# One hybrid block in split fp32: VectorE alone makes the mixer's low weight parts, with deeper weight buffers

## The chip, the core and the metric

The kernel runs on one core of a Trainium2 chip. The metric is the device time of one execution in microseconds. Before the change, three runs took 2448.56, 2450.65 and 2450.76 us; the median is 2450.65 us. The engines are called as the profile calls them: PE (TensorE), DVE (VectorE), ACT (ScalarE), POOL (GpSimd) and SP (the engine whose queue issues the transfers).

## The reference

One transformer block on 256 tokens of width 2048, all in fp32. A vector `c` gives shift, scale and gate for three sublayers: a gated feed-forward network (width 5632), a mixer, and a second feed-forward network. Each result is scaled by its gate, added to the scaled input and normalised. Cut to the core:

```
y = swiglu_ffn(x*(1+scale0)+shift0, ...);  x = layer_norm(ALPHA*x + 0.5*gate0*y)
y = hybrid_mixer(x*(1+scale1)+shift1, ...); x = layer_norm(ALPHA*x + gate1*y)
y = swiglu_ffn(x*(1+scale2)+shift2, ...);  x = layer_norm(ALPHA*x + 0.5*gate2*y)
```

The mixer has two branches. One is differential attention with 8 heads: two softmax maps per head, the second subtracted with a factor. The other is a gated delta rule with 8 heads: a short convolution, a triangular system per chunk of tokens, and a state carried from chunk to chunk. Two gates merge the branches before a last projection.

## The kernel before

**Split products.** Every large weight matrix comes from memory in chunks of 128x1024 fp32 (512 KB, 4 KB in each partition of SBUF). Such a raw chunk `raw` is split into a high part `hi`, which ACT writes by rounding, and a low part `lo = raw - hi`, which is one subtraction of two SBUF tiles (`_split`, lines 177 to 198). Activations are kept as two parts in the same way (`h_hi`, `h_lo`). A product is then three matmuls: hi by hi, lo of the activation by hi, and hi of the activation by lo (`mm3`, lines 145 to 149; L147, L148 and L149 in the profile). One chunk feeds 24 such matmuls of 256 columns, or 12 of 512.

**Buffers.** `RAWB` raw chunks (5) and `WB` pairs of part buffers (3) rotate. `weights` (line 219) is called as PE's instructions for a chunk are written. It first has `ahead` issue the splits of the next `WB - 1` chunks and transfers up to `RAWB` chunks past the last split. A `hi` waits until PE has read the buffer's former content, and a transfer waits until both parts of the raw chunk that it overwrites are made.

**Who makes `lo`.** Line 193 chooses: with `pool_lo` 0 it is DVE, with 1 POOL, with 2 POOL for each even chunk. The value is 1 or 2 in the first visits of the start (`START_LO`), 1 at the change from one sublayer to the next, `POOL_LO` in the mixer (line 1298) and 0 elsewhere.

**The order.** It is written out when the program is built. The main stream of matmuls runs through, and small threads (a convolution, an attention head, a pair of delta-rule heads) put their steps between its products when a clock of the planner, `k.t`, has passed the time at which the planner expects the step's inputs. The planner counts what DVE, ACT and POOL have been given, each on a clock of its own (`_Engine`, lines 75 to 89). So moving an operation from one engine's count to another's also moves the steps of the threads. Each engine runs its instructions in the written order.

**The mixer.** Its main stream makes queries, keys, values, gates and projections (`MIXER_JOBS`, line 41). Beside it four pairs of delta-rule heads (`_delta_pair`) and eight attention heads (`_attn_head`) pass through DVE, ACT and PE in chains of many short steps. `_gates` (line 843) computes decay rates by a chain of small POOL operations (`pol`), then `sp` and `g` on DVE, and then PE multiplies `g` (`pG`). POOL also makes `kqd`, `yal` and `ybl`, the last two being low parts of the branches' results. The branch products that follow the mixer read `ybl`.

**The start.** PE's first visit needs two tiles of activations, which come from vectors of `w_ada` (`sar`) by DVE, ACT and POOL (`_h_tile`, line 493: `hf`, `h_hi`, `h_lo`).

Of the kernel before, what the change touches and what calls it, by code (L numbers as in the profile page):

```python
# [34 lines left out]
DEPTH = 3  # L35
PACE = 2.5
START_LO = (1, 1, 1, 2, 0, 0)
RAWB = 5
WB = 3
MARGIN = 0.9  # L40
MIXER_JOBS = [("d", 0), ("v", 0), ("d", 1), ("a", 0), ("d", 2), ("a", 1), ("d", 3), ("a", 2), ("a", 3)]
POOL_LO = 2
TAIL = 2
LAST_TAIL = 5
MORE0 = 12
# [46 lines left out]
class _Kernel:  # L92
    def __init__(self, tc):
# [10 lines left out]
        self.users = []  # L104
        self.depth = RAWB

# [62 lines left out]
    def _dma(self):  # L169
        i = self.nd  # L170
        self.came[i] = self.load(self.through.get(i - RAWB, 0.0))
        raw = self.rawp.tile([128, 1024], F32, tag="raw", name=f"raw{i}")
# [46 lines left out]
    def weights(self, held=0):  # L219
# [3 lines left out]
        i = self.nu  # L223
        upto, n = i, WB - 1 - held
        while n and upto + 1 < len(self.plan):
# [61 lines left out]
def _xstat(k, n, act, done, tail=0):  # L287
# [21 lines left out]

    more = max(0, tail - WB)  # L310
    if more:
# [975 lines left out]
def _mixer(k, a, h, pre, mk_ada, finish):  # L1287
    nc, tc = k.nc, k.tc
    acts = [h, h]
    with ExitStack() as mctx:  # L1290
# [5 lines left out]
        with tc.tile_pool(name="dp", bufs=1) as dp:  # L1296
            k.dp = dp
            k.pool_lo = POOL_LO
            dv = dp.tile([128, 2, 1024], F32, tag="dv", name="dv")
# [80 lines left out]
def _first_h(k, a, h, hp):  # L1380
# [24 lines left out]
    for i, (f, half, kind) in enumerate(plan):  # L1405
# [13 lines left out]
        if half and kind:  # L1419
# [8 lines left out]
            if f == 3:  # L1428
                k.depth = RAWB


@with_exitstack
def tile_hybrid_block(ctx: ExitStack, tc: tile.TileContext, names, aps):
# [6 lines left out]
    k.pp = pp = ctx.enter_context(tc.tile_pool(name="pp", bufs=1))  # L1440
    k.rawp = ctx.enter_context(tc.tile_pool(name="rawp", bufs=RAWB))
    k.wp = ctx.enter_context(tc.tile_pool(name="wp", bufs=WB))
    k.smallp = ctx.enter_context(tc.tile_pool(name="smallp", bufs=2))
# [262 lines left out]
```

## Time and profile before

| | before |
|---|---|
| median of 3 runs | 2450.65 us |
| the profiled execution | 2450.7 us, span 2448.6 us |
| PE busy | 2341.9 us (96%) |
| DVE busy | 1718.0 us (70%) |
| ACT busy | 1038.1 us (42%) |
| POOL busy | 469.2 us (19%) |
| mean granted PE clock | 0.982 |
| read from memory | 572.98 MB |

The span runs from the first to the last instruction. The stages, by time from the span's start: first feed-forward network to about 790 us, mixer proper about 826 to 1321, branch products and projection to about 1663, second feed-forward network to the end. An engine's busy share is a mean over these stages. A wait is put down to the instruction that ended it.

### The profile page before, as it was taken

The numbers are of one execution on the slowest core, as the hardware profiler recorded it, in microseconds if no ns is written. First come the engines' busy times: TensorE is split into PE (matmuls) and PEld (weight loads), VectorE is DVE, ScalarE is ACT, GpSimd is POOL, SyncE is SP. The second block draws the span as 40 slices with busy tenths as digits, with TensorE's granted clock in tenths as the row PEclk, the third lists the DMA queues.
The fourth block names the chain that finished last, engine by engine and source line by source line (L and its number), as shares of the span: only waits on it lengthen the run. The fifth ranks groups of instructions, "written<-read, shape, count | busy, mean of one in ns | idle before, by whom it ended". The sixth has DMA issues, their size and how long they took to land. (4 is left out here: it accounts for less than half of the span.)

```text
span 2448.6 us, 42378 instructions
## 1 busy us (share of the span) xinstructions
PE 2341.9 (96%) x16989; PEld 2218.5 (91%) x16989; DVE 1718.0 (70%) x2480; ACT 1038.1 (42%) x1420; POOL 469.2 (19%) x276
## 2 busy tenths in 40 slices
PE   7999989999999899989899999998999999999997
PEld 7999987899998779888789999988999988999987
DVE  5767887877765676987876887786786555444456
ACT  4434444344444445444443434444434433444433
POOL 6883000000002532342422210013040000000001
PEclk8999999999999999999999999999999999999999
DMA  9998878998865555444446888875888555555553
GB/s 366 337 332 295 296 237 280 319 335 302 301 219 179 194 175 188 143 164 148 149 151 232 297 305 295 292 273 196 295 310 274 193 194 190 182 186 184 182 194 123
DMA packets 166380, 582.05 MB, mean 238 GB/s; under 512 B 19820, under 2 KB 22812, under 8 KB 165416
## 3 DMA queue, kind: packets, MB, share of 16 engines
q1 hardware_dynamic: 166184, 579.36, 68.1%
q8 instruction: 133, 2.18, 0.4%
q14 instruction: 63, 0.52, 0.1%
HBM read 572.98 MB, written 7.88 MB: 237 GB/s over the span
## 5 line engine op out<-in xcount | busy, mean ns | idle before, releaser
L88 ACT ACTIVATE hi<-raw 128x1024 fp32r<-128x1024 f32 x768 | 811.4, 1059 | 1012.9 <-PE mm L148 406.0
L88 DVE TENSOR_TENSOR lo<-raw,hi 128x1024 fp32r<-128x1024 f32 x631 | 790.2, 1255 | 534.5 <-ACT hi L88 532.6
L149 PE MATMUL mm<-h_hi,lo 128*128 128x256 f32 x3072 | 868.7, 283 | 16.5 <-DVE lo L88 16.4
L147 PE MATMUL mm<-h_hi,hi 128*128 128x256 f32 x3072 | 880.6, 287 | 0.0
L148 PE MATMUL mm<-h_lo,hi 128*128 128x256 f32 x3072 | 871.2, 284 | 0.0
L149 PEld LDWEIGHTS mm<-h_hi,lo 128*128 128x128 f32 x3072 | 585.8, 191 | 18.6 <-DVE lo L88 18.1
L147 PEld LDWEIGHTS mm<-h_hi,hi 128*128 128x128 f32 x3072 | 581.7, 189 | 3.1 <-issue 2.8
L148 PEld LDWEIGHTS mm<-h_lo,hi 128*128 128x128 f32 x3072 | 582.3, 190 | 1.2 <-issue 0.8
L88 POOL TENSOR_TENSOR lo<-raw,hi 128x1024 fp32r<-128x1024 f32 x137 | 337.5, 2470 | 1090.6 <-ACT hi L88 1080.3
L148 PE MATMUL mx<-lo,hid 128*128 128x512 f32 (+1 forms) x764 | 283.3, 371 | 1.5 <-DVE lo L88 1.5
L147 PE MATMUL mx<-hi,hid 128*128 128x512 f32 (+1 forms) x764 | 283.0, 370 | 1.6 <-ACT hi L88 1.6
L149 PE MATMUL mx<-hi,hid 128*128 128x512 f32 (+1 forms) x764 | 282.8, 370 | 0.0
L147 PE MATMUL mms<-h_hi,hi 128*128 128x256 f32 x896 | 253.5, 283 | 9.6 <-ACT hi L88 6.7
L149 PE MATMUL mms<-h_hi,lo 128*128 128x256 f32 x896 | 255.1, 285 | 2.9 <-POOL lo L88 1.6
L148 PE MATMUL mms<-h_lo,hi 128*128 128x256 f32 x896 | 255.1, 285 | 2.2 <-POOL h_lo L88 2.2
L147 PEld LDWEIGHTS mms<-h_hi,hi 128*128 128x128 f32 x896 | 171.6, 192 | 10.4 <-ACT hi L88 7.1
L149 PEld LDWEIGHTS mms<-h_hi,lo 128*128 128x128 f32 x896 | 170.0, 190 | 3.7 <-POOL lo L88 1.9
L148 PEld LDWEIGHTS mms<-h_lo,hi 128*128 128x128 f32 x896 | 169.6, 189 | 2.6 <-POOL h_lo L88 2.5
L147 PEld LDWEIGHTS mx<-hi,hid 128*128 128x128 f32 x764 | 144.0, 188 | 27.2 <-ACT hi L88 2.1
L148 PEld LDWEIGHTS mx<-lo,hid 128*128 128x128 f32 x764 | 143.9, 188 | 26.8 <-DVE lo L88 2.5
L149 PEld LDWEIGHTS mx<-hi,hid 128*128 128x128 f32 x764 | 144.0, 188 | 24.6
L88 DVE SCALAR_TENSOR_TENSOR acc<-ar,cs,acc 128x512 f32<-128x512 f32 x180 | 147.3, 818 | 8.5 <-DMA ar<-in_w_gate_dram 5.0
(295 smaller groups left out, 2530.8 us busy)
## 6 DMA issues: line engine op xcount, KB each, us to landing
raw<-in_w_ffn_in_dram SPq DMA_DIRECT2D x240, 512.0 KB, 4.3
raw<-in_w_ffn_out_dram SPq DMA_DIRECT2D x176, 512.0 KB, 4.1
raw<-in_w_first_dram SPq DMA_DIRECT2D x112, 512.0 KB, 4.8
ar<-in_w_gate_dram SPq DMA_DIRECT2D x96, 512.0 KB, 4.7
ar<-in_w_ada_dram SPq DMA_DIRECT2D x96, 512.0 KB, 4.9
sar<-in_w_ada_dram SPq DMA_DIRECT2D x64, 512.0 KB, 6.0
raw<-in_w_gab_dram SPq DMA_DIRECT2D x64, 512.0 KB, 4.2
raw<-in_w_kq_dram SPq DMA_DIRECT2D x32, 512.0 KB, 3.5
```

Of the source, the lines that this page charges most:

```text
L88: return f(*args, **kw)
L147: mm(ps, lhsT=lhs[0], rhs=rhs[0], start=start, stop=False, skip_group_check=True)
L148: mm(ps, lhsT=lhs[0], rhs=rhs[1], start=False, stop=False, skip_group_check=True)
L149: mm(ps, lhsT=lhs[1], rhs=rhs[0], start=False, stop=stop, skip_group_check=True)
```

## The change

Four numbers. `POOL_LO` goes from 2 to 0, so that in the mixer DVE makes every low part. `WB` goes from 3 to 4 and `RAWB` from 5 to 6. The scratch for descriptors of dynamic transfers is set to 1024 bytes at the program's construction, where the default was used; the two further buffers take 12 KB in each partition.

```
-RAWB = 5
-WB = 3
+RAWB = 6
+WB = 4
...
-POOL_LO = 2
+POOL_LO = 0
...
-    nc = _bacc.Bacc("TRN2", target_bir_lowering=False, num_devices=1)
+    nc = _bacc.Bacc("TRN2", target_bir_lowering=False, num_devices=1, dynamic_dma_scratch_size=1024)
```

The number of POOL instructions falls by 58 and that of DVE grows by 58; in the mixer it is 59, and at the start POOL gets one more. No other instruction is added or removed, but many stand elsewhere.

POOL at the start; `h_lo` is the low part of a tile of activations, `lo` that of a weight chunk. Before:

```order
L88 TENSOR_TENSOR h_lo_89<-hf_178,h_hi_88 128x256
L88 TENSOR_TENSOR lo_185<-raw_165,hi_184 128x1024
L88 TENSOR_TENSOR lo_191<-raw_170,hi_190 128x1024
L88 TENSOR_TENSOR lo_199<-raw_182,hi_198 128x1024
L88 TENSOR_TENSOR h_lo_89<-hf_224,h_hi_88 128x256
L88 TENSOR_TENSOR lo_256<-raw_188,hi_255 128x1024
```

and now:

```order
L88 TENSOR_TENSOR h_lo_89<-hf_178,h_hi_88 128x256
L88 TENSOR_TENSOR lo_185<-raw_165,hi_184 128x1024
L88 TENSOR_TENSOR lo_191<-raw_170,hi_190 128x1024
L88 TENSOR_TENSOR lo_199<-raw_182,hi_198 128x1024
L88 TENSOR_TENSOR lo_205<-raw_188,hi_204 128x1024
L88 TENSOR_TENSOR h_lo_89<-hf_230,h_hi_88 128x256
```

A fourth weight part stands ahead of the second tile's `h_lo`; on ACT its `hi` stands ahead of that tile's `h_hi` likewise.

DVE early in the mixer, where `_gates` ends (`raw` with `ada` is a product of vectors, `v` a convolution, `pG` is PE's). Before:

```order
L88 SCALAR_TENSOR_TENSOR kq_1_8960<-th_9207,kq_1_8960 128x512
L88 ISA raw_9041,ada_9088<-raw_9041,crow,tmp_9089 128x1024
L88 ISA ada_9088 128x1
L88 TENSOR_SCALAR beta<-beta 128x16
L88 SCALAR_TENSOR_TENSOR sp<-xx,pol 128x16
L88 SCALAR_TENSOR_TENSOR g<-sp,ea 128x16
L88 SCALAR_TENSOR_TENSOR v_0_9219<-mm_9036,convw,v_0_9219 128x255 x2
L88 COPY G<-pG 128x16
```

and now:

```order
L88 TENSOR_TENSOR lo_9180<-raw_9012,hi_9179 128x1024
L88 SCALAR_TENSOR_TENSOR kq_1_8968<-th_9229,kq_1_8968 128x512
L88 TENSOR_TENSOR lo_9234<-raw_9048,hi_9233 128x1024
L88 SCALAR_TENSOR_TENSOR v_0_9227<-mm_9044,convw,v_0_9227 128x255 x2
L88 TENSOR_TENSOR lo_9256<-raw_9054,hi_9255 128x1024
L88 TENSOR_SCALAR beta<-beta 128x16
L88 SCALAR_TENSOR_TENSOR sp<-xx,pol 128x16
L88 SCALAR_TENSOR_TENSOR g<-sp,ea 128x16
```

Low parts now stand between the small steps. On PE, `pG` stands 18 matmuls of 512 columns further on in the main stream.

POOL late in the mixer (`yal` is an attention head's low part, `ybl` that of a pair of delta-rule heads). Before:

```order
L88 TENSOR_TENSOR lo_13894<-raw_13689,hi_13893 128x1024
L88 TENSOR_TENSOR lo_14000<-raw_13794,hi_13999 128x1024
L88 TENSOR_TENSOR ybl<-nz_3_13459,ybh 128x512
L88 TENSOR_TENSOR lo_14041<-raw_13891,hi_14040 128x1024
L88 TENSOR_TENSOR yal<-yf_14011,yah 128x256
L88 TENSOR_TENSOR lo_14135<-raw_13965,hi_14134 128x1024
L88 TENSOR_TENSOR yal<-yf_14176,yah 128x256
```

and now:

```order
L88 TENSOR_TENSOR yal<-yf_13522,yah 128x256
L88 TENSOR_TENSOR yal<-yf_13758,yah 128x256
L88 TENSOR_TENSOR yal<-yf_13964,yah 128x256
L88 TENSOR_TENSOR yal<-yf_14200,yah 128x256
L88 TENSOR_TENSOR ybl<-nz_3_13410,ybh 128x512
```

The weight parts are gone from POOL, and the last `ybl` stands behind the last `yal`. On PE the delta rule's steps stand later in the main stream: the second pair's by up to 252 main matmuls, and the last pair's last transposes 87 main matmuls before the branch products where they stood 282 before them.

## Rows read from the trace of the kernel before

**Rows 1.** Windows: start:end length, then busy us of each engine, clock, DMA.
```profile
1700.00:1800.00 100.00, 100.00 (x833) 99.92 (x833) 72.58 (x85) 44.56 (x57) 6.90 (x5) 1.00 0.84 287
826.00:1321.00 495.00, 451.37 (x3409) 425.72 (x3408) 380.18 (x816) 216.84 (x432) 182.44 (x106) 0.97 0.48 164
300.00:370.00 70.00, 60.53 (x439) 56.14 (x438) 62.22 (x95) 32.78 (x57) 0.00 (x0) 0.98 0.74 245
```

**Rows 2.** What PE waited for, 826 to 1321: us, times, longest.
```profile
PE mm L149 <- DVE lo L88: 15.5, 7, 4.6
PE pG L153 <- DVE g L88: 6.9, 1, 6.9
PE UY L153 <- DVE mn L88: 4.1, 1, 4.1
```

**Rows 3.** Groups by form on DVE, 826 to 1321: busy us, mean ns, idle before.
```profile
L88 DVE TENSOR_TENSOR lo<-raw,hi 128x1024 fp32r<-128x1024 f32 x60 | 83.6, 1394 | 50.8 <-ACT hi L88 50.8
L88 DVE TENSOR_TENSOR U<-U,UY 128x512 f32<-128x512 f32 x20 | 13.3, 684 | 2.6 <-PE UY L153 1.9 <-ACT hi L88 0.6
L88 DVE TENSOR_SCALAR r<-r,lam 128x2 f32<-128x2 f32 x8 | 7.8, 977 | 0.3
```

**Rows 4.** The same view on POOL, 826 to 1321.
```profile
L88 POOL TENSOR_TENSOR lo<-raw,hi 128x1024 fp32r<-128x1024 f32 x59 | 149.9, 2542 | 291.8 <-ACT hi L88 281.6 <-PE sc L153 10.2
```

**Rows 5.** The same view on DVE, 1950 to 2350, where POOL is idle.
```profile
L88 DVE TENSOR_TENSOR lo<-raw,hi 128x1024 fp32r<-128x1024 f32 x142 | 174.0, 1226 | 197.7 <-ACT hi L88 197.7
```

**Rows 6.** Instructions in order of time around 851: start, us, engine, idle before.
```profile
850.89 4.63 POOL L88 TENSOR_TENSOR lo<-raw,hi 128x1024 fp32r<-128x1024 f32 x2
850.96 2.29 DVE L88 SCALAR_TENSOR_TENSOR sp<-xx,pol 128x16 f32<-128x16 f32 x1 [1.94 <-POOL pol L88]
853.29 2.26 DVE L88 SCALAR_TENSOR_TENSOR g<-sp,ea 128x16 f32<-128x16 f32 x1
```

**Rows 7.** The same view around 1172.
```profile
1169.60 0.16 DVE L88 SCALAR_TENSOR_TENSOR d_ft<-d_ft,msq 128x4 f32<-128x4 f32 x1
1169.78 2.38 POOL L88 TENSOR_TENSOR lo<-raw,hi 128x1024 fp32r<-128x1024 f32 x1 [2.62 <-ACT hi L88]
1169.80 2.38 DVE L88 SCALAR_TENSOR_TENSOR fa<-d_ft,fa 128x4 f32<-128x4 f32 x1
...
1172.89 2.42 POOL L88 TENSOR_TENSOR lo<-raw,hi 128x1024 fp32r<-128x1024 f32 x1 [0.72 <-ACT hi L88]
1173.03 3.36 DVE L88 TENSOR_TENSOR lo<-raw,hi 128x1024 fp32r<-128x1024 f32 x1
...
1176.44 0.58 PE L149 MATMUL mm<-h_hi,lo 128*128 128x256 f32 x1 [4.65 <-DVE lo L88]
```

**Rows 8.** The same view: the first and the last held instruction of DVE.
```profile
837.26 1.30 DVE L88 SCALAR_TENSOR_TENSOR e<-xx 128x16 f32<-128x16 f32 x1
...
1290.79 1.37 DVE L88 TENSOR_SCALAR ae<-ae,r 128x128 f32<-128x128 f32 x1
```

**Rows 9.** What PE waited for, 300 to 370.
```profile
PE aps L153 <- ACT acchi L88: 3.7, 2, 3.0
PE mx L148 <- DVE lo L88: 1.5, 2, 0.8
```

**Rows 10.** Instructions in order of time at the start.
```profile
20.74 1.06 ACT L88 ACTIVATE hi<-raw 128x1024 fp32r<-128x1024 f32 x1 [2.68 <-DMA raw<-in_w_first_dram]
...
21.70 0.40 ACT L88 ACTIVATE h_hi<-hf 128x256 fp32r<-128x256 f32 x1
21.87 2.34 POOL L88 TENSOR_TENSOR lo<-raw,hi 128x1024 fp32r<-128x1024 f32 x1 [1.37 <-ACT hi L88]
...
24.17 0.72 POOL L88 TENSOR_TENSOR h_lo<-hf,h_hi 128x256 fp32r<-128x256 f32 x1
24.95 0.58 PE L148 MATMUL mms<-h_lo,hi 128*128 128x256 f32 x1 [2.21 <-POOL h_lo L88]
```

**Rows 11.** DMA queues, whole span: packets, MB, share of 16 engines.
```profile
q1 hardware_dynamic: 166184, 579.36, 68.1%
```

## The prediction, made before the changed kernel ran

> **What bounds the kernel now.** I read the windows first, to find where PE loses time. In an undisturbed stretch PE is busy throughout and does 833 matmuls in 100 us, so one of 256 columns costs 0.120 us, at full clock [rows 1]. Outside the mixer most windows look like that one. The mixer does not: of its 495 us PE is busy 451.4, so 43.6 are idle, and its granted clock averages 0.97. With two levels, 2.4 and 1.2 GHz, a mean of 0.97 is 6% of the time at the lower one, and costs 0.03 x 495 = 14.9 us of work. What the mixer can give back by shorter waits is therefore at most 43.6 + 14.9 = 58.5 us. DVE is busy 380.2 us there, 77%, and POOL 182.4.
>
> Second, the waits. PE's 43.6 us in the mixer divide into 15.5 for low weight parts from DVE, 6.9 for `g`, and 21.2 for other steps of the chains, the longest 4.1 [rows 2].
>
> Third, the durations, which tell why DVE is late. Where POOL is idle a `lo` takes DVE 1.226 us [rows 5]; in the mixer the same form has a mean of 1.394 [rows 3]. The order of time shows the reason. `sp` and `g` work on 16 columns and took 2.29 and 2.26 us, while two of POOL's `lo` ran [rows 6]. Around 1172 a step of 4 columns took 0.16 us, and an equal one, begun 0.02 us after a POOL `lo`, took 2.38, as long as that `lo`; next a DVE `lo` took 3.36 beside another, and PE stood 4.65 us [rows 7]. So a DVE instruction that meets a POOL `lo` is held to its end. Between 826 and 1321, 43 DVE instructions beside one took over 0.15 us more than their form does elsewhere, the first at 837, the last at 1291 [rows 8], in sum 77 us. `U<-U,UY`, which reads one operand from PSUM, isn't among them: its mean is 684 ns [rows 3].
>
> The Trainium skill says it as a rule (page "SBUF — State Buffer", section "Who interferes with whom"): GpSimd's port pair is VectorE's second, taken as an exclusive lock for an instruction, and a VectorE instruction with two SBUF inputs needs it against a GpSimd instruction that reads SBUF. The trace agrees (2.38 us beside 2.38). By the rule what is held now would go wholly with those POOL instructions, and DVE's sum below would fall as worked out there.
>
> **The low parts in the mixer.** POOL loses 59 `lo`, 149.9 us [rows 4]. DVE gains 59 x 1.226 = 72.3 us [rows 5] and loses up to 77 of holding, so its busy time goes from 380.2 to about 375.5: no more than before. What changes is when it is late: no step of 0.2 us takes 2.3 any more, except beside POOL's remaining small operations.
>
> **The fourth pair.** The `hi` of a chunk still waits for the same event, PE's last use of an older chunk, since both the buffer it overwrites and the point at which it is issued move by one. But PE wants it one chunk later: 24 matmuls, 24 x 0.120 = 2.9 us more slack for each `lo`. The longest wait, 4.6, has 2.2 + 2.1 of holding in it [rows 7], so with 2.9 more it goes. I count all 15.5.
>
> **`pG`.** `sp` and `g` lose some 2.1 us each, and `pG` stands 18 matmuls of 512 columns later (an estimate from the 0.120 for half the columns: 18 x 0.24, some 4 us). Against that, three `lo` stand before `sp` now, 3.7 us, where a vector product stood; DVE had 1.94 us idle there [rows 6]. The 6.9 goes.
>
> **The other chain steps.** Of their 21.2 us I take two thirds, 14.1. The longest, 4.1 [rows 2], had one held instruction before it; and the order puts the steps later in the main stream than before, by up to 252 matmuls, 30 us. One third stays, since these chains also wait on ACT and PE themselves.
>
> Idle time falls by 15.5 + 6.9 + 14.1 = 36.5. The half-clock time I let fall in proportion: 14.9 x 36.5/43.6 = 12.5.
>
> **What DVE's queue costs.** Nothing before shows 59 more `lo` among chain steps. From below it is 0, because the planner now counts them on DVE's clock and places PE's steps accordingly. From above: 77 us of holding went with 36.5 of idle time that I remove, so 72.3 us of new work, if as unlucky, brings back 34. I take 6, near the lower end, as the nearest row is the undisturbed stretch, where DVE is 73% busy and PE has no idle time [rows 1]. Mixer: -36.5 - 12.5 + 6 = -43.
>
> **300 to 370 us.** PE loses 9.5 idle and 0.02 x 70 = 1.4 of clock; DVE is busy 62.2 of 70 [rows 1]. Waits for `acchi` (3.7) and `lo` are the largest [rows 9]. The two sum products (`aps`) stand 51 and 66 main matmuls later, 6 to 8 us, and the `lo` come a chunk earlier in DVE's queue; but DVE's work is the same and it is nearly full. Bounds 0 and -10.9; I take -5.
>
> **The start.** ACT's third `hi` waited for its raw chunk until 20.74, and `h_hi` followed at 21.70 [rows 10]. Now a fourth `hi` is ahead of `h_hi`, and POOL has a fourth `lo`, 2.34 us, ahead of `h_lo`, for which PE waits until 24.95: +2.4. POOL's lag ends it: were the fourth chunk's landing later still, +4. It isn't won back, since PE has no idle time in the following visits.
>
> **At nothing.** The sixth raw chunk only keeps the transfers' distance, as splits run one chunk earlier. The small scratch: SP issues all transfers, on a hardware queue with 579.36 MB [rows 11]; if the size did touch it, the first stage would suffer, and no row bounds that. The changes between sublayers keep ACT's order. In the last tail, the last chunk's split waits for the same matmuls as before.
>
> Sum: -43 - 5 + 2.4 = -45.6, against the profiled execution's 2450.7, which is the median of the runs (2450.65) within 0.1: about **2406 us**. Its own range is 2390 to 2426, from the bounds of the chain steps (two thirds, give or take one third: 7 us, with clock 10) and of DVE's queue.
>
> **Rivals.**
>
> *Given back at the mixer's end.* The last pair's transposes stood 282 main matmuls before the branch products, 34 us; now 87, 10.4 us. Behind them come a product on DVE, `ybh` on ACT and `ybl` on POOL, which the branch products read. If the chain runs further behind the planner than those 10.4 us allow, PE stands there. For it: the planner puts DVE's small steps at 0.08 us plus a little per column, where those of 4 columns take 0.16 [rows 7]. Against it: the held time that it never counted, 77 us, is gone. Price: half the mixer's gain, 22: 2428.
>
> *All of it.* The mixer's 58.5 and the 10.9 of 300 to 370 go, at +2.4: 2450.7 - 67 = 2384. Against it: the chains also depend on ACT and on PE's own order.
>
> *DVE becomes the mixer's bound (the slower side).* If the holding is not POOL's doing, it stays, and DVE needs 380.2 + 72.3 = 452.5 us. In 300 to 370 DVE was as good as full at 62.2/70 = 0.89 [rows 1]; at that share the mixer takes 452.5/0.89 = 508, 13 more than now: 2450.7 + 13 - 5 + 2.4 = 2461. It decides when less than 12 of the 77 us goes (440/0.89 = 495). Against it: two durations that equal POOL's to 0.02 us [rows 6, 7]. The Trainium skill's page "Perfetto Trace Analysis", section "Optimizing Scalar/DVE Operations", speaks for it: a saturated DVE may be helped by giving work to ScalarE or even GpSimd, the reverse of this change; the same paragraph warns that the shared port may spoil it. This trace shows the spoiling (2.38 us for 0.16).
>
> *No change.* The chains are bound by their own latency, and PE's waits move to other steps of the same pair: 2450.7 - 5 + 2.4 = 2448.
>
> **Chances.** Forecast 0.60, given back 0.15, all of it 0.13, no change 0.06, DVE-bound 0.06. A measurement of this kernel tells about 0.2% (5 us) from no change. Faster 0.88, the same 0.06, slower 0.06. The range that leaves out 2 in 10 is 2384 to 2436.
>
> **What will show it.** Right: in the mixer no DVE step of few columns takes over 1 us, but beside `kqd`, `yal` or `ybl`; DVE's `lo` has a mean near 1.23; DVE is busy about 375 us over a mixer of some 450; PE's waits for `lo` and `g` there are under 3 us together; the clock is at 0.99. At the start PE waits for the second `h_lo` until about 27. Wrong: holds as long as before with POOL idle (DVE-bound), or one long wait of PE for `ybl` before the branch products (given back). New waits for `lo` of some us in the mixer would mean that its queue costs more than 6.

## The result, and the profile after

The changed kernel takes 2417.03 us, the median of four runs (2416.54 to 2420.50), where the kernel before takes 2449.61 beside it (2447.17 to 2450.76). The ratio is 0.9863, with an interval of 0.9849 to 0.9878. The forecast was 2406, with a range of 2384 to 2436. The mechanism was right; the gain was 33 us instead of 45.

The profiled execution took 2417.4 us, with a span of 2415.6, against 2450.7 and 2448.6. To find where the 33 us went I measured both traces at the same events of PE: the first product that follows the first feed-forward network (`pre`), the first branch product (which reads `yah`), and the next normalisation's transpose (`lnt`).

| us | before | after | difference |
|---|---|---|---|
| start to `pre` | 796.7 | 799.5 | +2.8 |
| mixer | 524.3 | 490.6 | -33.7 |
| branches and projection | 345.3 | 342.7 | -2.6 |
| second feed-forward network | 782.0 | 782.6 | +0.6 |

The windows of the trace after, with the columns of [rows 1]: the mixer between the same two events as the 495 us there, the stretch from 300 us, and the branches.

```profile
828.60:1290.40 461.80, 441.98 (x3413) 421.97 (x3412) 373.19 (x875) 215.37 (x432) 33.11 (x47) 0.98 0.52 175
300.00:380.00 80.00, 72.34 (x511) 67.70 (x509) 70.24 (x105) 36.73 (x60) 0.00 (x0) 0.96 0.76 248
1290.10:1632.80 342.70, 335.07 (x2508) 322.09 (x2506) 275.04 (x331) 139.06 (x157) 44.86 (x23) 1.00 0.83 291
```

In the first row DVE has 59 instructions more than before and is busy 7 us less (373.2 against 380.2). PE's idle time is 461.8 - 442.0 = 19.8 us, where it was 43.6. The waits that make it up, in the view of [rows 2]:

```profile
PE sc L153 <- ACT qkT L88: 4.0, 2, 3.4
PE mm L149 <- DVE lo L88: 3.5, 2, 2.9
PE pT L158 <- DVE ae L88: 3.0, 2, 2.6
PE av L153 <- DVE nz L88: 2.6, 1, 2.6
PE pT L158 <- DVE tm L88: 2.4, 1, 2.4
PE v L158 <- DVE v L88: 1.7, 2, 1.0
PE pG L153 <- DVE g L88: 1.0, 1, 1.0
```

Low weight parts fell from 15.5 us to 3.5, `g` from 6.9 to 1.0; the forecast had them under 3 together. The other steps of the chains fell only from 21.2 to 19.8 - 3.5 - 1.0 = 15.3. They are the top of the list now.

DVE's durations, by form in the mixer, as in [rows 3]:

```profile
L88 DVE TENSOR_TENSOR lo<-raw,hi 128x1024 fp32r<-128x1024 f32 x119 | 146.9, 1247 | 41.3 <-ACT hi L88 40.0 <-PE sc L153 1.0
L88 DVE TENSOR_TENSOR U<-U,UY 128x512 f32<-128x512 f32 x20 | 13.4, 684 | 6.4 <-PE UY L153 5.1 <-issue 1.1
```

A `lo` is back at 1.25 us, and `U<-U,UY`, which was never held, hasn't moved. The view of one tile, `r`, gives the least, median and longest duration in ns; the mean of this step was 977 [rows 3]:

```profile
L88 DVE TENSOR_SCALAR r<-r,lam x8: 228/228/229, 986.9 to 1257.5; 128x2 f32<-128x2 f32 x8
```

And the instructions in order of time where `_gates` ends, to be held against [rows 6]:

```profile
852.63 1.23 DVE L88 TENSOR_TENSOR lo<-raw,hi 128x1024 fp32r<-128x1024 f32 x1 [0.52 <-ACT hi L88]
853.77 0.17 DVE L88 TENSOR_SCALAR beta<-beta 128x16 f32<-128x16 f32 x1
856.27 0.18 DVE L88 SCALAR_TENSOR_TENSOR sp<-xx,pol 128x16 f32<-128x16 f32 x1 [2.33 <-POOL pol L88]
856.48 0.17 DVE L88 SCALAR_TENSOR_TENSOR g<-sp,ea 128x16 f32<-128x16 f32 x1
```

`sp` and `g` take 0.18 and 0.17 us where they took 2.29 and 2.26. Count a DVE instruction as held when it runs beside one of POOL's and takes over 0.15 us more than the median of its form in the kernel after. The held time in the mixer is then 4.3 us in 8 instructions, and 79.5 in 48 before. (The prediction's 77 us in 43 are those of them that stand beside a POOL `lo`; of these none is left.)

At the start, in order of time, against [rows 10]:

```profile
20.60 1.06 ACT L88 ACTIVATE hi<-raw 128x1024 fp32r<-128x1024 f32 x1 [2.66 <-DMA raw<-in_w_first_dram]
...
21.73 4.65 POOL L88 TENSOR_TENSOR lo<-raw,hi 128x1024 fp32r<-128x1024 f32 x2 [1.35 <-ACT hi L88]
21.87 1.06 ACT L88 ACTIVATE hi<-raw 128x1024 fp32r<-128x1024 f32 x1 [0.21 <-DMA raw<-in_w_first_dram]
22.83 0.40 ACT L88 ACTIVATE h_hi<-hf 128x256 fp32r<-128x256 f32 x1
...
23.29 0.58 PE L147 MATMUL mms<-h_hi,hi 128*128 128x256 f32 x1 [4.22 <-ACT h_hi L88]
...
26.35 0.72 POOL L88 TENSOR_TENSOR h_lo<-hf,h_hi 128x256 fp32r<-128x256 f32 x1
...
27.12 0.58 PE L148 MATMUL mms<-h_lo,hi 128*128 128x256 f32 x1 [3.25 <-POOL h_lo L88]
```

The fourth `hi` is ahead of `h_hi`, and two `lo` stand before `h_lo`. PE gets it at 27.12 instead of 24.95.

### The profile page after: what moved, and what is told of

Its sections match the earlier page's. It is cut to its first block, busy times and chain, and to the rows that moved or that the text cites. A ratio compares the mean times of both kernels' runs of the same rounds, so it can differ in the third digit from the quotient of the medians.

```text
span 2415.6 us, 42349 instructions
## 1 busy us (share of the span) xinstructions
PE 2331.5 (97%) x16989; PEld 2214.6 (92%) x16989; DVE 1708.3 (71%) x2538; ACT 1036.6 (43%) x1420; POOL 323.1 (13%) x218
## 4 chain that ended last, share of the span: by engine, by line
PE 87%; DVE 7%; issue 2%; ACT 1%; DMA 1%; POOL 1%; DVEq 0%; SPq 0%; ACTq 0%; POOLq 0%
PE mm L147 15%; PE mm L148 15%; PE mm L149 15%; PE mx L149 8%; PE mx L147 8%; PE mx L148 8%; PE mms L148 4%; PE mms L147 4%; PE mms L149 4%; DVE lo L88 2%; DVE acc L88 1%; PE UY L153 1%; DVE x L88 1%; ACT hi L88 1%; PE pre L148 1%
## 5 line engine op out<-in xcount | busy, mean ns | idle before, releaser
L88 DVE TENSOR_TENSOR lo<-raw,hi 128x1024 fp32r<-128x1024 f32 x690 | 855.2, 1245 | 524.6 <-ACT hi L88 516.8
L88 POOL TENSOR_TENSOR lo<-raw,hi 128x1024 fp32r<-128x1024 f32 x79 | 189.9, 2412 | 793.4 <-ACT hi L88 793.4
```

The source lines that it names most:

```text
L88: return f(*args, **kw)
```

## The experiments

Theory: POOL's low parts hold DVE, and ending that is nearly all of the gain; the rest of the change is small. The rivals were that the new written order or the deeper buffers bring it, that DVE's holding isn't POOL's doing, or that POOL's `lo` simply come later than DVE's would (2.54 us for 1.23). Against the last, PE waits for no `lo` of POOL's in the mixer before: every one of its waits for low parts there is for DVE's. The mixer column is the time between the two events of the table above, from each run's trace.

| run | pairs, raw chunks | order planned for | mixer's even `lo` made by | time, us | ratio to before, interval | mixer, us |
|---|---|---|---|---|---|---|
| before | 3, 5 | POOL | POOL | 2449.61 | 1 | 524.3 |
| e4 | 3, 5 | POOL | DVE | 2415.83 | 0.9860, 0.9846 to 0.9875 | 491.2 |
| e1 | 3, 5 | DVE | DVE | 2423.99 | 0.9898, 0.9881 to 0.9914 | 498.9 |
| e2 | 4, 6 | POOL | POOL | 2442.56 | 0.9972, 0.9961 to 0.9983 | 518.0 |
| e5 | 4, 6 | DVE | POOL | 2433.84 | 0.9937, 0.9922 to 0.9952 | 508.6 |
| after | 4, 6 | DVE | DVE | 2417.03 | 0.9863, 0.9849 to 0.9878 | 490.6 |
| e7 | 4, 6 | POOL | DVE | 2407.98 | 0.9828, 0.9812 to 0.9845 | 483.1 |

**e1_dve_only: one number of the change, the maker of the low parts.**

```
-POOL_LO = 2
+POOL_LO = 0
```

> POOL_LO is 0 as in the change; the buffers (5 raw chunks, 3 pairs) and the scratch are those of before. Holding theory (DVE late because it is held beside POOL's low parts; 77 us of held time is the cause of most of the mixer's lost PE time): nearly all of the gain is here, about 2422 us (before less 26, and without the 3 us that the start lost). Order theory (PE waits less because the planner, which now counts these low parts on DVE, places chain steps later): the same here, about 2422. Slack theory (the fourth pair is what takes the waits for low parts away): at most 10 us of gain, about 2440, with waits of PE for lo in the mixer of 12 us or more.

Measured: 2423.99 us, so this alone gives three quarters of the change's gain. Its mixer, in the columns of [rows 1]:

```profile
826.00:1300.00 474.00, 449.03 (x3445) 427.09 (x3445) 374.47 (x876) 219.69 (x435) 33.97 (x47) 0.97 0.53 173
```

PE is idle 25.0 us there, 8.2 of it for low parts in two places (7.0 and 1.2), where the changed kernel, with its fourth pair, has 3.5.

**e2_buffers_only: the change without that number.**

```
-POOL_LO = 0
+POOL_LO = 2
```

> Four pairs, six raw chunks and the small scratch as in the change; POOL still makes each even low part in the mixer. Holding theory: held DVE time stays near 77 us; only PE's waits for lo (15.5 us) shrink, by about two thirds with their clock, against +3 at the start: about 2440. Order theory: the planner's counts are those of before, so about 2446. Slack theory: most of the gain, 2420 to 2425.

Measured: 2442.56. The mixer gains 6.3 us and the start loses 3 (the main stream's 200th matmul at 52.5 us, where it is 49.3 before). DVE is held as before, 79.9 us in 50 instructions.

**e3_scratch_only: the small scratch alone.**

```
-    nc = _bacc.Bacc("TRN2", target_bir_lowering=False, num_devices=1)
+    nc = _bacc.Bacc("TRN2", target_bir_lowering=False, num_devices=1, dynamic_dma_scratch_size=1024)
```

> The kernel before with the scratch for dynamic descriptors at 1024 bytes and nothing else; every engine's order is that of before. Theory (the scratch costs and gains nothing, since SP issues the transfers on a hardware queue): 2450 us, ratio 1.000 within 0.002. Rival (a part of the change's 33 us comes from the scratch, for instance by other tile addresses or by fewer bytes to set up at the start): below 2445.

Measured: ratio 0.9996, interval 0.9986 to 1.0006. It costs and gains nothing that can be measured.

**e4_old_order_dve: only who executes.** The planner still counts the even parts on POOL, so that PE, ACT and SP have the order of before to the last row. In the mixer the instruction itself goes to DVE, at the place where it is written.

```
-        eng.tensor_tensor(lo, raw, hi.bitcast(F32), ALU.subtract)
+        (_As(eng, self.nc.vector) if self.in_mixer else eng).tensor_tensor(
+            lo, raw, hi.bitcast(F32), ALU.subtract)
```

(`_As` sets the engine for the length of the call.)

> Buffers and written order of before to the last instruction, but in the mixer the low parts that stood on POOL are executed by DVE, at the same place in the order; the planner still counts them on POOL. Holding theory: held time falls to under 5 us and DVE's busy time in the mixer stays at about 375 us; PE's idle time there falls from 43.6 to about 22: 2425. Order theory: chain steps stand where they stood and DVE has 59 more instructions that the planner did not count: no gain or a loss, 2445 to 2460. Slack theory: 2450, with more waits for lo.

Measured: 2415.83, as fast as the whole change.

```profile
826.00:1288.00 462.00, 440.58 (x3409) 417.82 (x3408) 371.51 (x875) 216.85 (x432) 33.23 (x47) 0.99 0.55 176
```

DVE does 59 instructions more in 8.7 us less [rows 1]; 4.0 us of it is held. Nothing but the executing engine differs, so that alone gives 34 us; whether by the end of the holding is what e8 and e9 ask. PE is idle 21.4 us here. Of it 8.1 are for low parts and 3.4 for `g`, so the other steps of the chains have 9.9, where the changed kernel has 15.3. Set beside e1, it also shows what the planner's new count does by itself: +8.2 us.

**e5_new_order_pool: the reverse.** The changed kernel with its order, but in the mixer POOL executes the even parts (held time 71.1 us in 55 instructions).

```
-        eng.tensor_tensor(lo, raw, hi.bitcast(F32), ALU.subtract)
+        (_As(eng, self.nc.gpsimd) if self.in_mixer and i % 2 == 0 else eng).tensor_tensor(
+            lo, raw, hi.bitcast(F32), ALU.subtract)
```

> Buffers and written order of the changed kernel to the last instruction, but in the mixer each even chunk's low part is executed by POOL again, at the same place in the order; the planner counts it on DVE. Holding theory: held DVE time is back at 60 to 80 us, and most of the gain is lost: about 2440. Order theory: chain steps stand late enough for held steps too: 2417 to 2424. Slack theory: 2417 to 2422.

Measured: 2433.84, 16.8 us above the changed kernel and 8.7 below e2. About half of the gain is lost, not most of it. So where DVE is held, the order planned for DVE is the better one, by 9 us; where it isn't, it is the worse one, by 8.2 with three pairs (e1 against e4) and 10.0 with four (e6 against e7, below, which share their start). In these runs a plan that expects DVE late paid only where DVE was late.

**e6_start_kept: the old look-ahead at the start, up to the fourth tile of activations.**

```
-        upto, n = i, WB - 1 - held
+        upto, n = i, (2 if self.first else WB - 1) - held
...
-        self.depth = RAWB
+        self.depth, self.first = 5, True
...
             if f == 3:
-                k.depth = RAWB
+                k.depth, k.first = RAWB, False
```

> The changed kernel, but until the second tiles of activations are made only 2 chunks are split ahead and 5 raw chunks loaded ahead, as before the change; from then on 3 and 6. If the start's loss comes from the fourth weight part ahead of the second h_hi and h_lo, PE passes its 20th matmul 3 us earlier and the whole is 3.3 us shorter: 2413.7. Rival: the time is given back where DVE is full (300 to 370 us), so 2416 to 2417.

Measured: 2417.95, no gain. The main stream is only 0.7 us behind before up to 109 us. There the look-ahead has been let go, further splits stand ahead of a later tile's `h_hi`, and PE waits from 60 to 130 us as follows, where it waits for neither in the other two traces:

```profile
PE mms L147 <- ACT h_hi L88: 2.0, 1, 2.0
PE mms L148 <- POOL h_lo L88: 0.4, 1, 0.4
```

After them it is 4.9 us behind. The same loss came later.

**e7_old_order_buffers: the buffers of the change, the start of e6, the mixer planned as for POOL and executed on DVE** (the edits of e6 and e4, and `POOL_LO = 2`).

> The written order of before in the mixer (the planner counts each even low part on POOL), executed by DVE, with four pairs, six raw chunks, the small scratch, and the start's look-ahead of before. The order alone cost 8 us at three pairs (2424.0 against 2415.8). If that is a cost of placing the chain steps too late, it stays with four pairs: 2415.8 less the 7 to 10 us that the buffers gave in the mixer, about 2407. Rival: the fourth pair and the order answer to the same waits, and with four pairs the order does not matter: about 2413, as the changed kernel with its start mended.

Measured: 2407.98, the fastest version, 9 us below the change.

```profile
826.00:1285.00 459.00, 444.63 (x3452) 423.19 (x3451) 372.33 (x877) 217.21 (x434) 33.95 (x47) 0.99 0.55 179
```

PE is idle 14.4 us there, and no wait for low weight parts is left in its list. Against e4 the deeper buffers give 491.2 - 483.1 = 8.1 us of the mixer, both planned for POOL. Against e2, which has these buffers and in the mixer this written order, only who executes differs, and the mixer is 518.0 - 483.1 = 34.9 us shorter: e4's 33.1 once more, with four pairs.

**e8_pool_reads: the holding put back, with nothing depending on it.** e4 with the small scratch, and on POOL, wherever it made a low part, a copy of one column of that chunk's `hi` (to begin at the same event) and then this, which no one reads or waits for:

```
+        k.nc.gpsimd.tensor_copy(k.pace, hi[:, 0:1].bitcast(F32))
+        k.nc.gpsimd.tensor_tensor(k.idle, k.idle, k.idle, ALU.subtract)
```

> Buffers and order of before with the mixer's low parts on DVE (2415.8), the small scratch, and 59 more instructions on POOL that nobody waits for: behind each even hi a copy of one column, then a subtraction of a 128x1024 tile from itself (two reads of SBUF, one write, about as long as a low part). If POOL's reading alone holds DVE, no matter for what data, DVE's small steps take up to 2.4 us again and 15 to 30 us come back: 2430 to 2446. If what cost time was that PE waited for POOL's slow results, nothing comes back: 2415 to 2419.

Measured: 2483.38, ratio 1.0141 (1.0118 to 1.0163): 33 us slower than before, more than expected. The window of its mixer:

```profile
826.00:1354.00 528.00, 460.45 (x3408) 432.39 (x3407) 438.35 (x875) 216.24 (x432) 190.43 (x165) 0.95 0.48 154
```

By form, first on POOL, then on DVE:

```profile
L1727 POOL TENSOR_TENSOR idle<-idle 128x1024 f32<-128x1024 f32 x59 | 121.6, 2061 | 0.2 <-POOL pace L1726 0.2
```

```profile
L88 DVE TENSOR_TENSOR lo<-raw,hi 128x1024 fp32r<-128x1024 f32 x119 | 172.2, 1458 | 48.3 <-ACT hi L88 48.2
```

DVE's instructions are those of e4 and take 67 us longer (438.4 after 371.5); counted as above, 70.7 us of them is held. `g`, 0.17 us long in e4, ends with POOL's idle subtraction, at 856.97 and 856.94:

```profile
855.05 1.89 POOL L1727 TENSOR_TENSOR idle<-idle 128x1024 f32<-128x1024 f32 x1
855.21 1.76 DVE L88 SCALAR_TENSOR_TENSOR g<-sp,ea 128x16 f32<-128x16 f32 x1
```

POOL's own steps (`kqd`, `ybl` and others) also queue behind these 59, so e8 alone doesn't show that it is the reads. e9 has about the same queue.

**e9_pool_writes: the same, but POOL only writes.** In place of the subtraction, two memsets of the idle tile:

```
-        k.nc.gpsimd.tensor_tensor(k.idle, k.idle, k.idle, ALU.subtract)
+        [k.nc.gpsimd.memset(k.idle, 0.0) for _ in range(2)]
```

> As the run before, but instead of the subtraction POOL writes zeros twice into the 128x1024 tile (no read of SBUF, about 1 us each). If only POOL's reads hold a DVE instruction with two SBUF inputs, little comes back: 2416 to 2421. If any use of POOL's port holds DVE, a part in proportion to POOL's busy time comes back: 2428 to 2440.

Measured: 2424.18, between the two forecasts. POOL is as busy as in e8 within 14 us, and the mixer is 498.1 us, not 557.4.

```profile
826.00:1295.00 469.00, 443.93 (x3410) 419.94 (x3409) 379.31 (x875) 216.72 (x432) 176.73 (x224) 0.99 0.54 173
```

```profile
L1727 POOL MEMSET idle<- 128x1024 f32 x118 | 112.5, 953 | 3.4
L1726 POOL COPY pace<-hi 128x1 f32<-128x1 f32 x59 | 36.1, 612 | 269.1 <-ACT hi L88 269.1
```

The held time is 14.0 us in 25 instructions, against 70.7 in 56. What is left isn't mainly the 59 copies, although they read; the trace separates it by the kind of DVE's step. Of the instructions that began while a memset ran, all 31 `lo` took as long as alone, within 0.01 us, and so did the 59 other TENSOR_TENSOR steps. But 15 of 17 TENSOR_SCALAR steps, which work on one tile, were held to the memset's end, 8.0 us in sum. In order of time (the second memset ends at 1213.29):

```profile
1211.28 1.22 DVE L88 TENSOR_TENSOR lo<-raw,hi 128x1024 fp32r<-128x1024 f32 x1
1211.33 1.96 POOL L1727 MEMSET idle<- 128x1024 f32 x2
1212.62 0.69 DVE L88 TENSOR_SCALAR r<-r,lam 128x2 f32<-128x2 f32 x1
```

`r`, 0.228 us alone, ends at 1213.31. Of the other 6 us, e4 has 4.0 too, beside POOL's own steps. So for DVE's instructions with two tiles in SBUF it isn't that POOL is busy, but that it reads; its steps on one tile are held by POOL's writes as well.

The Trainium skill draws that line in "SBUF — State Buffer", section "Who interferes with whom": a VectorE instruction with two SBUF inputs meets a GpSimd instruction that reads SBUF, but not one that only writes. For these instructions the two runs agree (e8: 20 of 23 `lo` that began during an idle subtraction were held; e9: none of 31).

**e10_start_shallow: e7 with the old look-ahead until the start's last activation tile is made.**

```
             if f == 3:
-                k.depth, k.first = RAWB, False
+                k.depth = 5
...
                         k.wait(lambda: first.done)
-                        first = None
+                        first, k.first, k.depth = None, False, RAWB
```

> The changed buffers with the mixer planned as if POOL made its even low parts while DVE makes them, and at the start the old look-ahead of two chunks and five raw chunks until the last activation tile of the start is made (the run that kept them only up to the fourth tile lost 4.2 us near 109 us). Up to the end of the start every engine has the order of before. Theory (the start's loss is ACT's and POOL's queue, nothing else): PE has no wait for h_hi or h_lo between 60 and 130 us, the start's offset against before stays under 1 us, and the time is some 3 to 4 us below that run's 2408: 2404. Rival (the loss is given back later, at 220 to 380 us, where the deeper buffers now begin to fill): 2407 to 2409.

Measured: 2408.85 (ratio 0.9826, 0.9813 to 0.9840), the same as e7. The wait near 109 us is gone, and the main stream is 1.3 us behind before up to 314 us. Then it loses 2.3: from 300 to 380 us PE waits for the gate's sum products,

```profile
PE aps L153 <- ACT acchi L88: 9.6, 2, 6.4
```

where the change has 4.4, and it arrives at 417 us with +3.7 (e7: +4.4). The rival on record was right: the start's gain is given back later. What sets the moment at which `acchi` is ready, DVE's sums before it or the loads they use, wasn't taken apart.

## Why the prediction was right, and where its sizes were off

**The holding.** Right, and shown: e4 changes the executing engine alone and gives 34 us; e8 puts reads back on POOL that nobody waits for, and takes more than that away; e9 keeps POOL as busy without most reads and takes 8. That the whole change gives no more than e4 is a balance: the deeper buffers gain about what the new order and the longer start lose. DVE's busy time in the mixer came out at 373.2 us for 375.5.

**The mixer's sum.** Predicted -43, measured -33.2 between the windows of [rows 1] and of after. By its terms:

| term | predicted, us | measured, us |
|---|---|---|
| waits for low parts | -15.5 | -12.0 |
| wait for `g` | -6.9 | -5.9 |
| other chain steps | -14.1 | -5.9 |
| work at the lower clock (measured: PE's busy time) | -12.5 | -9.4 |
| DVE's longer queue | +6 | (in the rows above) |

The 9.4 is PE's busy time, 451.4 to 442.0. By the traces' clock records the work lost at the lower clock is 15.4 us before and 8.5 after, so 6.8 of the 9.4 are the clock's, and the cause of the rest is open. The queue's cost has no row of its own: it is a part of what remains in the others, 3.5 us for low parts among it, and no run separates it. The term that is most off is the *other chain steps*: "two thirds" went, by my estimate, and 28% did. I had two reasons for it. The first, that steps are no longer held, is right: in e4, with the order of before, the steps fall from 21.2 to 9.9. The second, that the new order puts the steps later and so gives them more slack, has the wrong sign here: e1 against e4 and e6 against e7 show that this order costs 8 to 10 us once DVE isn't held. With the old order and the same buffers (e7) the mixer gains 41.2, close to the 43 that I predicted for the new one. That the fourth pair takes all waits for low parts, which I had counted, holds in e7 (none, from 8.1 in e4) and not quite in the changed kernel (3.5).

Where it costs can be seen by counting PE's main matmuls. At the 6650th (1014 us in the changed kernel) the change is 25.0 us ahead of before and e7 10.2; at the 7100th (1107 us) it is 11.5 ahead and e7 15.2. e5, with the change's order and held, goes from 16.5 to 3.2 over the same 450. Most of that swing is work put off, and no loss: up to the 6650th PE has done 80 steps of the chains fewer than before, and in the next 450 matmuls it does 181 where it did 113, and is busy 82.5 us for 72.5. What is lost there is idle time: 10.5 us, for 7.0 before and 2.6 in e7. The 7.9 us over e7 are about what the order costs. PE waits there first 2.9 us for a `lo` (until 1020), then 3.4 for `qkT` (until 1076) and 2.6 for `ae` (until 1095). Whether the later ones follow from the first wasn't separated.

**The clock.** 0.98 for the predicted 0.99. Two neighbouring windows show the cost of one wait:

```profile
1010.00:1020.00 10.00, 7.17 (x61) 6.96 (x59) 9.52 (x28) 0.00 (x0) 0.00 (x0) 0.96 0.32 110
1020.00:1030.00 10.00, 9.88 (x62) 9.88 (x63) 7.62 (x11) 7.60 (x15) 0.74 (x1) 0.70 0.76 261
```

PE was idle 2.8 us in the first, and in the second it is busy nearly throughout, at a granted clock of 0.70, and does 62 matmuls where its neighbour at 1030 does 88. That the clock's term goes with the idle time was a rough rule: 55% of the idle time went, and 6.8 of 15.4 us of the work at the lower clock, which is 44%.

**300 to 370 us.** Predicted -5, measured -1.4 (the offset to before goes from +4.2 to +2.8 between 232 and 417 us). I counted 6 to 8 us of slack from the later place of the sum products. That was misread as well: the two that wait in this stretch stand 66 and 36 main matmuls later (the 51 belongs to one at 285 us, which doesn't wait). And PE still waits there:

```profile
PE aps L153 <- ACT acchi L88: 4.4, 2, 3.5
PE aps L153 <- DVE acclo L88: 1.1, 1, 1.1
```

[rows 9] had 3.7 for the first. This step failed: the input comes later as well. The first `acchi` of the stretch was made at 323.55 us before and is made at 336.20 now, and PE stood 3.0 us for it and stands 3.5. In e10, with the deeper buffers and the products where they stood before, the wait is 9.6.

**The start.** The two waits grew from 2.9 to 4.2 us and from 2.2 to 3.3, +2.4 together, as predicted, and `h_lo` was there at 27.12 for "about 27". The clock wasn't in the sum: over the first 40 us it fell from 0.83 to 0.74, and the stream is 3.3 us behind from there on. That such a loss isn't won back, since PE is busy in the visits that follow, was right for the change (+3.3, and +2.8 at 417 us); e6 and e10 add that taking it away gains nothing either, since a later step waits.

**At nothing.** Right for the scratch (e3). The branches came out 2.6 us shorter, which I had not forecast; PE is idle 7.6 us there for 9.1 and busy 1.1 less. e3, with every instruction where it is before, is 1.1 shorter there too, so at most 1.5 is the change's.

**The rivals.** *Given back at the mixer's end* did not come: the last `ybl` ends at 1287.88, and PE reads it at 1290.83 without a wait. But of the 10.4 us of room between the last transposes and that product only some 3 were left when `ybl` was made. *All of it* missed the same 15.3 us of chain steps that I overrated. *DVE becomes the bound* fell with its reason: all 77 held us beside POOL's `lo` went (4.3 remain beside its other steps), where it needed fewer than 12. e8 is that rival made real, and I had priced it too low: 2461 at a share of 0.89 for DVE, where the mixer of e8 reaches 438.4/528 = 0.83 and the kernel takes 2483. The Trainium skill's page "Perfetto Trace Analysis", section "Optimizing Scalar/DVE Operations", spoke for this rival with its advice to unload a saturated engine; its own warning about the shared port is what decided, as DVE's 380.2 and 373.2 us show.

## What to carry to other kernels

Before moving work from VectorE to GpSimd, look at the durations of VectorE's small instructions beside GpSimd's. Where they equal what is left of GpSimd's own, VectorE is held, and the move may save it nothing: here VectorE was busy 380.2 us with GpSimd's help and 373.2 without, and the chains of small steps were late besides. When a planner or a scheduler decides the order, separate who executes from who is counted: the two had opposite signs here, and the better version (2408 us) keeps the old order with the new engine. A wait that is removed early is worth something only if no later step takes the time back, as one did in e6 and in e10.

## What the runs showed of the hardware

A microsecond of holding doesn't have one price. From the ratios and the held times: before against e4, 34 us for 75.5 held; e5 against after, 18 for 67; e8 against e4, 69 for 67. It is about one where VectorE has all the low parts in both runs. In the first two pairs the end of the holding comes together with 59 more `lo` for VectorE, so 0.45 and 0.27 are net of that work; that the written order makes the difference between these two is argued and not shown.

GpSimd is held as well. With nothing but small operations left in the changed kernel, its steps still vary (least, median and longest ns):

```profile
L88 POOL TENSOR_TENSOR pol<-pol,s x8: 222/224/1082, 848.6 to 856.0; 128x16 f32<-128x16 f32 x8
L88 POOL TENSOR_TENSOR kqd<-kq,eG x8: 455/461/1449, 878.5 to 1181.3; 128x128 f32<-128x128 f32 x8
```

The longest `pol`, 1.08 us for 0.22, began at 848.56 beside a VectorE `lo` that ran from 848.35 to 849.56, and ended at 849.64. It lies in the chain for which `sp` waited 2.33 us. VectorE's sum products of 1024 columns (`raw` with `ada`), with several operands in SBUF, are held like the subtractions: a mean of 1.28 us in the changed kernel and 1.45 to 1.48 in e8.
